# A hybrid GLA / Fourier encoder layer on one core: weight splits, scans, head fillers and the end of the scan stage in another order

## Chip, core and metric

One NeuronCore of a Trainium2 chip runs the whole layer for one sequence of 2048 positions. The metric is the device time of one execution in microseconds (us); lower is better. "The clock" is the clock that TensorE was granted, as the profile shows it, as a share of full speed.

## What is computed

```
proj = x @ w_in                      # 2048 x 1024 by 1024 x 2592, split into
q, k, v, gf_lr, gb_lr, z_gla, u, z_fnet
# A) gated linear attention, 4 heads, forward and backward, chunked; per direction
log_a = log_sigmoid(g_lr @ w_gate_up + b_gate) / 16
S_t = diag(a_t) S_{t-1} + k_t^T v_t ;  o_t = q_t S_t        # o = o_fwd + o_bwd
o = o * rsqrt(mean(o^2) + eps) * gla_norm_g * silu(z_gla)
# B) Fourier mixing: real part of the 2-D DFT over (positions, group channels)
f = real(fft2(u)) @ w_fnet * silu(z_fnet)
y = concat(o, f) @ w_out
out = layernorm(alpha * x + y, ln_g, ln_b)
```

Everything is float32. The kernel splits each large operand into a high and a low part of TensorE's fast format (`split`: a cast on ScalarE for the high part, a subtraction on VectorE for the low part) and makes three products.

## The kernel before, in words

The first stages (z_gla, u, z_fnet, the transform, q and k) end at about 397 us of the span and are not touched. Two stages follow.

**The scan stage** (`phase3`) goes through 8 blocks `b` of 256 positions, two chunks `t` of 128 each. For each block TensorE makes 96 products of x with the weights of v and the gate ranks (`pw_part`, `pv_part`: line L94), transposes the two rank tiles `rn` (`gate_t`, L813, one per chunk), and makes the gates from the transposed tile R (`gates`, L825). ScalarE and VectorE then make log-sigmoid (L827, L829, L837, L838), two running sums over positions, which are the scans of the stage's name here (`gates1`, L843 and L845 on VectorE), and from those the decays (`gates2`: small copies from L855, difference L859, clip L860, exponentials L862 and L863) that scale q (L879) and k (L880, `scaled`). With scaled q and k of the block before, `gla_a` makes the scores (L889, L890), transposes k (L893), masks the scores (L895, L896 on VectorE) and copies k back (`ks`, L898 on ScalarE); `gla_b` makes the state increments (L908, copied to `S` by L910 and L912) and the inner outputs (L915, copied by L919). The state chain over chunks runs on GpSimd (`chain_f`, `chain_step`, L1144 and L1147). x of the next block is loaded (L76) and split (`xhl`, L55 on ScalarE and L58 on VectorE).

**The last stage** (`phase4`) goes through the 16 chunks `n` from 15 down to 0: `prep` (state product L1214, squares, split `shl`), `norm` (mean square by two products L1228 and L1229, L1231 and L1232, then L1233 and the output gate L1235, split into `mix`), the output product `outp` (L1168: 24 products of 512 columns with the second half of w_out, tile wB, over the Fourier part that `p4_head` splits; 24 with the first half, tile wA) and `finish` (layer norm and store; its last step, L1264, is on GpSimd).

The second half of w_out is loaded and split in four pieces while the scan stage runs: `wof_load` is a generator, one `next(wof)` in each of blocks 2 to 6, which splits the piece loaded before and loads the next one. At the end of the scan stage `p4_start` splits the heads of chunks 15 and 14 and loads and splits the first half of w_out (`load_w`), and the Fourier part of chunk 15's output product fills the waits of `gla_a` and `gla_b` of the last block.

Each engine works through its own queue in order. The queues' order comes from the order of the code and from a scheduler that sorts by it; `after(ev)` and `issue_after` put what is inside behind the named instruction on that instruction's own engine. PSUM tiles come from rings: `mm` with 4 buffers, `pa` and `pg` with 2 each.

```
if 1 < b < 7:
    with after(self.x_dma, self.oi_ev, self.sc_ev):
        next(wof)
```

Of the kernel before, what the change touches and what calls it, by code (L numbers as in the profile page):

```python
# [43 lines left out]
class Kern:  # L44
# [7 lines left out]
    def split(self, hi, lo, src, lo_eng=None, hi_eng=None):  # L52
        nc = self.nc
        if hi_eng is None:
            nc.scalar.copy(out=hi, in_=src)  # L55
        else:
            hi_eng.tensor_copy(out=hi, in_=src)
        (lo_eng or nc.vector).tensor_tensor(out=lo, in0=src, in1=f32(hi), op=ALU.subtract)  # L58
# [12 lines left out]
    def load_x(self, b, lo_eng=None):  # L71
        nc = self.nc
        halves = []
        for hf in range(2):
# [3 lines left out]
            self.split(t[:, 0], t[:, 1], raw, lo_eng)  # L78
# [672 lines left out]
    def phase3(self):  # L751
# [16 lines left out]
        with ExitStack() as ctx:  # L768
# [82 lines left out]
            def gates2(b, blk):  # L851
# [8 lines left out]
                V.tensor_scalar(out=g8, in0=g8, scalar1=-CAP, scalar2=CAP, op0=ALU.max, op1=ALU.min)  # L860
# [22 lines left out]
            def gla_a(b, t, blk):  # L883
                q, k = blk["q"], blk["k"]
# [7 lines left out]
                for h in range(4):  # L892
                    nc.tensor.transpose(kt[:, h], k[:, h, ts_], ident)  # L893
                at = gp.tile([P, 4, P], F32, name="at", tag="at", bufs=2)
                V.tensor_tensor(out=at, in0=af, in1=mf.rearrange("p (o i) -> p o i", o=1).broadcast_to([P, 4, P]), op=ALU.mult)  # L895
                self.at_ev = V.copy_predicated(at.rearrange("p h i -> p (h i)"), mb, ab.rearrange("p h i -> p (h i)"))  # L896
                ks = gp.tile([P, 4, P], F32, name="ks", tag="ks", bufs=2)
                self.ks_ev = nc.scalar.copy(out=ks, in_=kt)  # L898
# [44 lines left out]
            for b in range(NBLK):  # L943
# [27 lines left out]
                if b == 1:  # L971
                    with after(R_ev):
                        gates2(0, prev)
                gates(b, blk)
# [46 lines left out]
    def p4_start(self, last=None):  # L1021
# [9 lines left out]
        self.wog = self.load_w("wA", a["w_out"][:, 0:4], 4, 1024)  # L1031

    def wof_load(self):
        nc = self.nc
        w = self.wof = self.wpool.tile([P, 2, 4, 1024], F32R, name="wB_w", tag="wB")
        todo = []
        for k in range(5):
            for raw, k0, c in todo:
                self.split(w[:, 0, k0, c:c + 512], w[:, 1, k0, c:c + 512], raw)
            todo = []  # L1040
            for c in (0, 512) if k < 4 else ():
# [129 lines left out]
    def phase4(self):  # L1171
        nc, a = self.nc, self.a
        V = nc.vector
        with ExitStack() as ctx:
# [12 lines left out]
            def prep(n):  # L1187
# [4 lines left out]
                d = self.blks[b]  # L1192
                if "zg" not in d:
# [11 lines left out]
                fuse = n == NCH - 1 and "op" in d  # L1205
# [20 lines left out]
            def norm(c):  # L1226
# [8 lines left out]
                zgm[c["n"]] = (V if c["n"] == NCH - 1 else nc.gpsimd).tensor_tensor(out=zg, in0=o3, in1=zg, op=ALU.mult)  # L1235
# [100 lines left out]
```

## Time and profile before

| what | value |
|---|---|
| median of 3 runs | 805.22 us (803.11 to 806.51) |
| the profiled execution | 803.78 us, span 802.0 us |
| TensorE (PE) busy | 754.5 us, 94% of the span |
| VectorE (DVE) busy | 545.2 us, 68% |
| ScalarE (ACT) busy | 382.4 us, 48% |
| GpSimd (POOL) busy | 199.4 us, 25% |
| mean granted clock | 0.986 |

The span runs from the first to the last instruction; the rest of the execution's time lies around it. Busy shares are means over stages: TensorE is full in most stages, and the idle time lies in the scan stage and at its end. Times in the rows below are us from the span's start.

### The profile page before, as it was taken

Reading aid. Unit: us, or ns where it says so; the run is one execution under the profiler, and the core shown is the slowest. Engines: PE = TensorE matmul, PEld = TensorE weight load, DVE = VectorE, ACT = ScalarE, POOL = GpSimd, SP = SyncE. Lnnn points to the kernel's source line nnn. Section 1 sums busy time; section 2 is a strip of 40 time slices with the busy share of each in tenths; the row PEclk is TensorE's granted clock in tenths of the full one; section 3 lists DMA queues with packets and bytes.
Section 4 is the critical chain, followed back from the end, with each engine's and each line's share of the span. In section 5 each row is a group of like instructions: output and inputs, shape, how many; then the busy total and the mean of one; then the engine's idle time right before and its main releaser. Section 6 shows DMA issues by size and latency. Waiting matters only on the chain.

```text
span 802.0 us, 13525 instructions
## 1 busy us (share of the span) xinstructions
PE 754.5 (94%) x5254; PEld 698.1 (87%) x5254; DVE 545.2 (68%) x802; ACT 382.4 (48%) x705; POOL 199.4 (25%) x139
## 2 busy tenths in 40 slices
PE   6999999999999998999998988899798999999994
PEld 6988899999999998999997888899677788888884
DVE  4692458555535989876576877878776767776764
ACT  6674352323224534445355776666755344334331
POOL 0000003020201000411302422432533654544431
PEclk9999999999999999999999999899999999999998
DMA  8875452443236782646764755434357445445321
GB/s 242 264 217 183 126 167 92 135 128 123 88 109 186 239 283 94 193 143 223 224 177 134 208 159 180 129 129 142 106 182 264 157 164 178 160 148 165 115 92 61
DMA packets 81407, 130.48 MB, mean 163 GB/s; under 512 B 7507, under 2 KB 55123, under 8 KB 81334
## 3 DMA queue, kind: packets, MB, share of 16 engines
q1 hardware_dynamic: 79030, 125.34, 49.4%
q10 hardware_dynamic: 2304, 4.20, 1.4%
q8 instruction: 43, 0.70, 0.4%
q14 instruction: 30, 0.25, 0.1%
HBM read 92.81 MB, written 36.70 MB: 161 GB/s over the span
## 4 chain that ended last, share of the span: by engine, by line
PE 62%; DVE 17%; ACT 9%; DMA 6%; issue 3%; POOL 2%; SPq 1%; DVEq 0%; ACTq 0%; POOLq 0%
PE mm L374 19%; PE mm L1168 19%; PE mm L291 5%; PE mm L86 4%; PE mm L94 3%; DVE c L845 3%; DVE c L843 2%; DVE fw L534 2%; DMA fw<-u_d 2%; PE pa L635 2%; PE pa L1214 1%; DVE fw L531 1%; PE pg L291 1%; PE pa L291 1%; PE mm L231 1%
## 5 line engine op out<-in xcount | busy, mean ns | idle before, releaser
L94 PE MATMUL mm<-wA_w,xhl 128*128 128x272 f32 x768 | 110.1, 300 | 0.0
L94 PEld LDWEIGHTS mm<-wA_w,xhl 128*128 128x128 f32 x768 | 103.2, 197 | 0.0
L86 PE MATMUL mm<-xhl,wC_w 128*128 128x256 f32 x768 | 96.0, 284 | 0.0
L1168 PE MATMUL mm<-wA_w,mix 128*128 128x512 f32 (+1 forms) x396 | 93.3, 385 | 2.7 <-ACT mix L55 1.6
L86 PEld LDWEIGHTS mm<-xhl,wC_w 128*128 128x128 f32 x768 | 93.7, 192 | 0.5 <-issue 0.5
L1168 PE MATMUL mm<-wB_w,mix 128*128 128x512 f32 (+1 forms) x396 | 92.3, 387 | 1.6 <-DVE mix L58 1.6
L1168 PEld LDWEIGHTS mm<-wA_w,mix 128*128 128x128 f32 x396 | 72.3, 188 | 19.2 <-ACT mix L55 2.6
L1144 POOL TENSOR_TENSOR S<-S 64x512 f32<-64x512 f32 x30 | 51.5, 1718 | 137.2 <-ACT S L910 135.4
L1168 PEld LDWEIGHTS mm<-wB_w,mix 128*128 128x128 f32 x396 | 71.5, 188 | 15.4 <-DVE mix L58 2.0
L58 DVE TENSOR_TENSOR xhl<-xraw,xhl 128x1024 fp32r<-128x1024 f32 (+1 forms) x52 | 58.0, 1118 | 27.2 <-ACT xhl L55 27.0
L55 ACT CAST xhl<-xraw 128x1024 fp32r<-128x1024 f32 (+1 forms) x52 | 49.3, 951 | 38.0 <-DMA xraw<-in_xt_dram 17.9
L55 ACT CAST x<-xraw 128x1024 fp32r<-128x1024 f32 x28 | 29.3, 1049 | 69.2 <-PE mm L374 56.9
L436 POOL TENSOR_TENSOR t<-t,t 128x512 f32<-128x512 f32 x7 | 10.8, 1556 | 190.2 <-DVE t L428 122.2
L58 DVE TENSOR_TENSOR x<-xraw,x 128x1024 fp32r<-128x1024 f32 x28 | 37.8, 1352 | 29.1 <-ACT x L55 29.1
L1264 POOL TENSOR_TENSOR r<-r,lnb 128x1024 f32<-128x1024 f32 x15 | 36.1, 2409 | 80.3 <-issue 56.7
L670 POOL TENSOR_TENSOR yf<-yf,zfl 128x256 f32<-128x256 f32 x24 | 21.5, 923 | 119.5 <-ACT yf L649 110.8
L374 PE MATMUL mm<-wC_s,x 128*128 128x256 f32 x384 | 48.2, 283 | 0.0
L1147 POOL TENSOR_TENSOR S<-S,alpha 64x512 f32<-64x512 f32 x30 | 47.4, 1580 | 2.7 <-ACT alpha L932 0.4
L374 PEld LDWEIGHTS mm<-wC_s,x 128*128 128x128 f32 x384 | 47.1, 192 | 0.1
L291 PE MATMUL mm<-xhl,wA_w 128*128 128x512 f32 x192 | 43.9, 389 | 0.0
L291 PEld LDWEIGHTS mm<-xhl,wA_w 128*128 128x128 f32 x192 | 36.0, 188 | 7.4
L55 ACT CAST mix<-zg 128x512 fp32r<-128x512 f32 x16 | 9.9, 622 | 57.2 <-POOL zg L1235 55.9
(202 smaller groups left out, 1489.2 us busy)
## 6 DMA issues: line engine op xcount, KB each, us to landing
xraw<-in_xt_dram SPq DMA_DIRECT2D x48, 512.0 KB, 4.6
xr<-in_x_dram SPq DMA_DIRECT2D x16, 512.0 KB, 3.8
out_dram<-r SPq DMA_DIRECT2D x15, 512.0 KB, 2.9
xraw<-in_xt_dram SPq DMA_DIRECT2D x24, 256.0 KB, 4.2
zg_d<-zs SPq DMA_DIRECT2D x32, 128.0 KB, 3.7
u_d<-t SPq DMA_DIRECT2D x16, 256.0 KB, 3.1
zf_d<-t SPq DMA_DIRECT2D x16, 256.0 KB, 2.5
zfl<-zf_d SPq DMA_DIRECT2D x32, 128.0 KB, 3.7
```

Source lines behind the costliest of these rows:

```text
L55: nc.scalar.copy(out=hi, in_=src)
L58: (lo_eng or nc.vector).tensor_tensor(out=lo, in0=src, in1=f32(hi), op=ALU.subtract)
L86: mm = self.nc.tensor.matmul(ps, w[:, s, k, c0:c0 + P], x[:, m, k % 4, :], start=(k == 0 and i == 0), stop=(k == KB - 1 and i == 2))
L94: self.nc.tensor.matmul(ps, x[:, s, k % 4, t * P:(t + 1) * P], w[:, m, k, c0:c0 + cols], start=(k == 0 and i == 0), stop=(k == KB - 1 and ...
L291: nc.tensor.matmul(ps[c], self.wzg[:, s, 2 * q + kk, c * P:(c + 1) * P], x[:, m, kk], start=(q == 0 and kk == 0 and j == 0), stop=(q == 3 ...
L374: nc.tensor.matmul(ps[:, i], s_[s][:, k, i * P:(i + 1) * P], m_[m][:, k], start=(k == 0 and j == 0), stop=(k == 3 and j == 2))
L670: (nc.gpsimd if g < 3 else nc.vector).tensor_tensor(out=yb, in0=yb, in1=zf, op=ALU.mult)
L845: V.tensor_tensor_scan(out=c2[64:128, ::-1], data0=r2[64:128, ::-1], data1=g2[64:128, ::-1], initial=0.0, op0=ALU.mult, op1=ALU.add)
L1144: E.tensor_tensor(out=S[ds, dst], in0=S[ds, dst], in1=S[ds, src], op=ALU.add)
L1147: E.tensor_tensor(out=d3, in0=d3, in1=al, op=ALU.mult)
L1168: nc.tensor.matmul(y, c["mix"][:, s, eb], w[:, v, eb % 4, lo:lo + m], start=(eb == 4 and i == 0), stop=(eb == 3 and i == 2))
L1264: nc.gpsimd.tensor_tensor(out=r, in0=r, in1=lnb, op=ALU.add)
```

## The change

Line numbers in this section are those of the file named with them. The parts of the change:

- `wof_load` now yields three times for a piece: after the load, after the two casts (ScalarE), after the two subtractions (VectorE). The load stands behind the x load of blocks 2 to 5, the casts behind the last `ks` copy at the head of blocks 3 to 6, the subtractions behind the x split of blocks 3 to 6.
- `gates1` (from L837 on) stands behind the masks and the `ks` copy of `gla_a(b-1, 0)`; in block 1 the first `gla_a` comes ahead of it.
- `gates2` is cut in two: `gates2` ends with the clip, `gates3` begins with the exponentials. `gla_a` is cut in two: `gla_s` (scores, transposes, `ks`), `gla_m` (masks).
- In block 7, where there is no next x to load, `p4_start` runs: the heads of chunks 15 and 14 are split there.
- The end of the scan stage: the Fourier part of chunk 15's output product comes first, the masks of chunk 13 stand behind the clip, the first half of w_out is loaded behind the last `ks` and the scaled k, half of chunk 14's Fourier part follows.
- In `phase4`: half of chunk 13's Fourier part is made early, into a `pa` buffer; chunk 15's gate tile is loaded early, into the free half of `oi`; chunk 14's output gate is on VectorE instead of GpSimd; for chunk 15 the square on ScalarE comes ahead of the copy on VectorE.

```diff
-                V.tensor_scalar(out=g8, in0=g8, scalar1=-CAP, scalar2=CAP, op0=ALU.max, op1=ALU.min)
+                self.clip_ev = V.tensor_scalar(out=g8, in0=g8, scalar1=-CAP, scalar2=CAP, op0=ALU.max, op1=ALU.min)
+
+            def gates3(b, blk):
+                g, c, g8, c8 = blk["gc"]
                 eq = c
...
             def gla_a(b, t, blk):
+                gla_s(b, t, blk)
+                gla_m(blk)
...
                 pw_part(xh, 0, blk)
                 if b > 1:
                     gla_b(b - 2, 0 if b == 2 else 1, old)
+                if 2 < b < 7:
+                    with after(self.ks_ev):
+                        next(wof)
...
-                if b + 1 < NBLK:
-                    with self.tc.issue_after(self.rn_ev.ins):
+                with after(self.rn_ev):
+                    if b + 1 < NBLK:
                         xn = self.load_x(b + 1)
-                if 1 < b < 7:
-                    with after(self.x_dma, self.oi_ev, self.sc_ev):
+                    else:
+                        self.p4_start(blk)
+                if 2 < b < 7:
+                    with after(self.x_lo):
+                        next(wof)
+                if 1 < b < 6:
+                    with after(self.x_dma):
                         next(wof)
...
                 if b > 1:
                     gla_a(b - 1, 0, prev)
-                if b == 1:
-                    with after(self.sc_ev):
+                    with after(self.ks_ev, self.at_ev):
                         gates1(b, blk)
-                else:
+                elif b == 0:
                     gates1(b, blk)
...
-                if b:
-                    gla_a(b - 1, min(b - 1, 1), prev)
+                if b == 1:
+                    gla_a(0, 0, prev)
+                    with after(self.ks_ev, self.at_ev):
+                        gates1(b, blk)
+                elif b:
+                    gla_s(b - 1, 1, prev)
+                    if b < NBLK - 1:
+                        gla_m(prev)
                 old, prev = prev, blk
             b = NBLK
-            with after(self.ks_ev, self.at_ev):
+            h15, h14 = self.head[NCH - 1], self.head[NCH - 2]
+            self.outp(h15, [4, 5, 6, 7], (0,))
+            with after(self.ks_ev):
                 gates2(b - 1, prev)
+            with after(self.clip_ev):
+                gla_m(old)
+            with after(self.ks_ev):
+                gates3(b - 1, prev)
+            self.outp(h15, [4, 5, 6, 7], (1,))
             gla_b(b - 2, 1, old)
             self.chain_f(2 * b - 3, 2 * b - 1)
-            with after(self.ks_ev):
-                self.p4_start(prev)
-            h15, h14 = self.head[NCH - 1], self.head[NCH - 2]
-            self.outp(h15, [4, 5, 6, 7], (0,))
             gla_a(b - 1, 0, prev)
-            self.outp(h15, [4, 5, 6, 7], (1,))
+            with after(self.sc_ev, self.ks_ev):
+                self.wog = self.load_w("wA", a["w_out"][:, 0:4], 4, 1024)
+            self.outp(h14, [4, 5, 6, 7], (0,))
             gla_a(b - 1, 1, prev)
             gla_b(b - 1, 0, prev)
+            nc.sync.dma_start(out=prev["oi"][:, 1].rearrange("p (h j) -> p h j", h=4), in_=self.zg_d[b - 1][:, :, P:2 * P])
...
-                zgm[c["n"]] = (V if c["n"] == NCH - 1 else nc.gpsimd).tensor_tensor(out=zg, in0=o3, in1=zg, op=ALU.mult)
+                zgm[c["n"]] = (V if c["n"] >= NCH - 2 else nc.gpsimd).tensor_tensor(out=zg, in0=o3, in1=zg, op=ALU.mult)
...
+            h13 = self.head[NCH - 3] = self.p4_head(NCH - 3)
+            self.outp(h13, [4, 5, 6, 7], (0,), get=self.pa)
             norm(cur)
```

The order of the built instructions, at three places.

**Blocks 3 to 6, VectorE.** The rows around the second rank tile: L880 scales k, L783 is the rank tile's low part, `wB_w` the w_out piece, `xhl` the x split, L811 belongs to R. Before:

```order
L880 TENSOR_TENSOR g<-kr,g 128x1024
L58 TENSOR_TENSOR wB_w<-wraw,wB_w 128x512 x2
L783 TENSOR_TENSOR rn<-mm,rn 128x32
L58 TENSOR_TENSOR xhl<-xraw,xhl 128x1024 x2
L811 MEMSET R 2x256
```

Of the change (L883 is the k scaling there, L1080 the subtraction of a w_out piece):

```order
L883 TENSOR_TENSOR g<-kr,g 128x1024
L783 TENSOR_TENSOR rn<-mm,rn 128x32
L58 TENSOR_TENSOR xhl<-xraw,xhl 128x1024 x2
L1080 TENSOR_TENSOR wB_w<-wraw,wB_w 128x512 x2
L811 MEMSET R 2x256
```

The two subtractions went from ahead of the rank tile to behind the x split. On ScalarE the two casts, which stood ahead of the rank tile's casts (L781, L782), now stand between the second `ks` copy and the small copies of the scan's results:

```order
L804 COPY v<-mm 128x272
L902 COPY ks<-pg 128x512
L1077 CAST wB_w<-wraw 128x512 x2
L855 COPY cmid<-c 128x8
L857 COPY cend<-c 64x8
```

**Block 1, VectorE.** The masks of chunk 0 (`at`) and the scans (`c`). Before:

```order
L880 TENSOR_TENSOR g<-kr,g 128x1024
L838 SCALAR_TENSOR_TENSOR g<-mm,g 128x512 x2
L895 TENSOR_TENSOR at<-pa,mf 128x512
L843 SCALAR_TENSOR_TENSOR c<-rst,g 64x1024
L845 SCALAR_TENSOR_TENSOR c<-rst,g 64x1024
L896 COPY_PREDICATED at<-mb,pa 128x512
L783 TENSOR_TENSOR rn<-mm,rn 128x32
```

Of the change (L908 and L909 are the masks there):

```order
L883 TENSOR_TENSOR g<-kr,g 128x1024
L908 TENSOR_TENSOR at<-pa,mf 128x512
L909 COPY_PREDICATED at<-mb,pa 128x512
L838 SCALAR_TENSOR_TENSOR g<-mm,g 128x512 x2
L843 SCALAR_TENSOR_TENSOR c<-rst,g 64x1024
L845 SCALAR_TENSOR_TENSOR c<-rst,g 64x1024
L783 TENSOR_TENSOR rn<-mm,rn 128x32
```

The second mask went from behind both scans to ahead of them. In blocks 2 to 7 both masks of chunk 0 stood ahead of the scans already.

**The end of the scan stage, TensorE**, from the last block's chunk 0 (`v,ks` and `at,v`) to the first norm (`shl,ones`). Before:

```order
L908 MATMUL pg<-v,ks 128x128 x4
L915 MATMUL pg<-at,v 128x128 x4
L1168 MATMUL mm<-wB_w,mix 128x512 x2
L1017 MATMUL pg<-fone,fm 1x1
L1168 MATMUL mm<-wB_w,mix 128x512 x2
L908 MATMUL pg<-v,ks 128x128 x4
L915 MATMUL pg<-at,v 128x128 x4
L1214 MATMUL pg<-qp,S 128x128 x4
L1168 MATMUL mm<-wB_w,mix 128x512 x19
L1228 MATMUL pg<-shl,ones 128x512
```

Of the change (L1204 is the output product there, L1252 the state product, L1266 the norm's):

```order
L919 MATMUL pg<-v,ks 128x128 x4
L926 MATMUL pg<-at,v 128x128 x4
L1204 MATMUL mm<-wB_w,mix 128x512 x7
L1049 MATMUL pg<-fone,fm 1x1
L1204 MATMUL mm<-wB_w,mix 128x512 x2
L919 MATMUL pg<-v,ks 128x128 x4
L926 MATMUL pg<-at,v 128x128 x4
L1204 MATMUL mm<-wB_w,mix 128x512 x3
L1252 MATMUL pg<-qp,S 128x128 x4
L1204 MATMUL pa<-wB_w,mix 128x512 x12
L1266 MATMUL pg<-shl,ones 128x512
```

Ahead of the first norm there are now 12 products of chunk 13 (`pa`) in place of 19 of chunks 15 and 14, which have moved further ahead: of the 48 of chunks 15 and 14, 36 stand ahead of the first row shown, against 25 before.

## Rows read from the trace of the kernel before

**Rows 1.** Windows between L813's starts: length, busy us of each engine, clock, DMA.

```profile
469.42:493.66 24.24, 21.31 (x175) 20.53 (x176) 18.78 (x24) 15.99 (x37) 8.37 (x4) 0.92 0.50 153
517.78:542.72 24.94, 22.57 (x175) 21.59 (x176) 18.65 (x24) 16.16 (x37) 7.80 (x4) 0.88 0.50 149
542.72:563.47 20.75, 19.91 (x175) 19.12 (x176) 16.96 (x21) 13.97 (x34) 7.58 (x4) 1.00 0.46 145
563.47:626.48 63.01, 55.06 (x345) 45.50 (x346) 45.87 (x66) 35.64 (x67) 28.59 (x19) 1.00 0.52 175
```

**Rows 2.** Timeline, TensorE at L813: start, length, instruction, idle before and releaser.

```profile
469.42 0.45 PE L813 MATMUL mm<-ident,rn 128*96 128x128 f32 x1 [3.15 <-DVE rn L783]
...
493.66 0.45 PE L813 MATMUL mm<-ident,rn 128*96 128x128 f32 x1 [2.93 <-DVE rn L783]
493.76 3.01 PE L94 MATMUL mm<-wA_w,xhl 128*128 128x272 f32 x12
...
542.72 0.32 PE L813 MATMUL mm<-ident,rn 128*96 128x128 f32 x1 [2.37 <-DVE rn L783]
542.79 1.76 PE L94 MATMUL mm<-wA_w,xhl 128*128 128x272 f32 x12
...
563.47 0.32 PE L813 MATMUL mm<-ident,rn 128*96 128x128 f32 x1 [0.84 <-DVE rn L783]
```

**Rows 3.** Timeline, ScalarE, VectorE and SyncE around L813 of block 4.

```profile
491.00 1.14 ACT L55 CAST wB_w<-wraw 128x512 fp32r<-128x512 f32 x2
491.65 1.85 DVE L58 TENSOR_TENSOR wB_w<-wraw,wB_w 128x512 fp32r<-128x512 f32 x2 [1.54 <-ACT wB_w L55]
493.42 0.18 DVE L783 TENSOR_TENSOR rn<-mm,rn 128x32 fp32r<-128x32 f32 x1
...
496.62 0.90 SPq L1043 DMA_DIRECT2D wraw<-in_w_out_dram  x2
```

**Rows 4.** Timeline, ScalarE and VectorE in block 6.

```profile
542.69 0.36 ACT L797 COPY v<-mm 128x240 f32<-128x240 f32 x1 [0.39 <-DVE rn L783]
542.95 1.05 ACT L55 CAST xhl<-xraw 128x1024 fp32r<-128x1024 f32 x1
544.04 1.23 DVE L58 TENSOR_TENSOR xhl<-xraw,xhl 128x1024 fp32r<-128x1024 f32 x1 [0.24 <-ACT xhl L55]
549.46 2.28 DVE L843 TENSOR_TENSOR_SCAN c<-rst,g 64x1024 f32<-64x1024 uint8 x1
553.24 0.59 ACT L898 COPY ks<-pg 128x512 f32<-128x512 f32 x1 [1.29 <-PE pg L893]
554.99 0.21 ACT L855 COPY cmid<-c 128x8 f32<-128x8 f32 x1 [1.16 <-DVE c L845]
563.00 0.19 ACT L782 CAST rn<-mm 128x32 fp32r<-128x32 f32 x1
```

**Rows 5.** The tile wB_w, blocks 3 to 6: ns min/median/max.

```profile
L58 DVE TENSOR_TENSOR wB_w<-wraw,wB_w x8: 676/956/1255, 467.4 to 541.9; 128x512 fp32r<-128x512 f32 x8
```

**Rows 6.** Timeline, VectorE and TensorE in block 1 and at L813 of block 2.

```profile
429.16 2.27 DVE L843 TENSOR_TENSOR_SCAN c<-rst,g 64x1024 f32<-64x1024 uint8 x1
433.77 0.73 DVE L896 COPY_PREDICATED at<-mb,pa 128x512 f32<-128x512 uint8 x1
434.64 1.61 PE L915 MATMUL pg<-at,v 128*128 128x128 f32 x8 [3.19 <-DVE rn L783]
442.84 0.38 PE L813 MATMUL mm<-ident,rn 128*96 128x128 f32 x2
```

**Rows 7.** Timeline, the end of the scan stage and the first chunks of the last.

```profile
580.65 2.14 DVE L58 TENSOR_TENSOR mix<-mf,mix 128x512 fp32r<-128x512 f32 x2
585.38 0.37 PE L889 MATMUL pa<-qp,g 64*128 64x128 f32 x1 [0.51 <-DVE g L880]
...
607.96 0.73 PE L1168 MATMUL mm<-wA_w,mix 128*128 128x512 f32 x2 [1.41 <-ACT mix L55]
```

**Rows 8.** The tile wraw, blocks 3 to 6: from issue to landing.

```profile
DMA to landing us min/median/max: 5.7/5.7/5.9
```

More of the change, by code (lines that the diff above doesn't have):

```diff
@@ L57, in split @@
             hi_eng.tensor_copy(out=hi, in_=src)
-        (lo_eng or nc.vector).tensor_tensor(out=lo, in0=src, in1=f32(hi), op=ALU.subtract)
+        return (lo_eng or nc.vector).tensor_tensor(out=lo, in0=src, in1=f32(hi), op=ALU.subtract)
     def load_w(self, tag, src, nkb, cols, eng=None):
@@ L77, in load_x @@
             t = self.xpool.tile([P, 2, 4, BLK], F32R, name="xhl", tag="xhl", bufs=4)
-            self.split(t[:, 0], t[:, 1], raw, lo_eng)
+            self.x_lo = self.split(t[:, 0], t[:, 1], raw, lo_eng)
             halves.append(t)
@@ L893, in gla_a, with gla_m @@
                     nc.tensor.transpose(kt[:, h], k[:, h, ts_], ident)
+                ks = gp.tile([P, 4, P], F32, name="ks", tag="ks", bufs=2)
+                self.ks_ev = nc.scalar.copy(out=ks, in_=kt)
+                blk["sc"] = af, ab, ks
+            def gla_m(blk):
+                af, ab, ks = blk.pop("sc")
                 at = gp.tile([P, 4, P], F32, name="at", tag="at", bufs=2)
@@ L896, in gla_a @@
                 self.at_ev = V.copy_predicated(at.rearrange("p h i -> p (h i)"), mb, ab.rearrange("p h i -> p (h i)"))
-                ks = gp.tile([P, 4, P], F32, name="ks", tag="ks", bufs=2)
-                self.ks_ev = nc.scalar.copy(out=ks, in_=kt)
                 blk["ak"].append((at, ks))
@@ L973, in phase3 @@
                         gates2(0, prev)
+                        gates3(0, prev)
                 gates(b, blk)
@@ L1030, in p4_start @@
         self.head = {n: self.p4_head(n) for n in (NCH - 1, NCH - 2)}
-        self.wog = self.load_w("wA", a["w_out"][:, 0:4], 4, 1024)
+        if not last:
+            self.wog = self.load_w("wA", a["w_out"][:, 0:4], 4, 1024)
     def wof_load(self):
@@ L1035, in wof_load @@
         w = self.wof = self.wpool.tile([P, 2, 4, 1024], F32R, name="wB_w", tag="wB")
[L1036 to L1041, printed above, removed]
+        for k in range(4):
+            raws = []
+            for c in (0, 512):
                 raw = self.xpool.tile([P, 512], F32, name="wraw", tag="wraw", bufs=4)
                 nc.sync.dma_start(out=raw, in_=self.a["w_out"][:, 4 + k, c:c + 512])
-                todo.append((raw, k, c))
+                raws.append((raw, w[:, 0, k, c:c + 512], w[:, 1, k, c:c + 512]))
+            yield
+            for raw, hi, lo in raws:
+                nc.scalar.copy(out=hi, in_=raw)
+            yield
+            for raw, hi, lo in raws:
+                nc.vector.tensor_tensor(out=lo, in0=raw, in1=f32(hi), op=ALU.subtract)
             yield
@@ L1163, in outp @@
         if ebs[0] >= 4:
-            c.setdefault("y", []).extend((self.mm([P, cuts[i][1]]), *cuts[i]) for i in halves)
+            c.setdefault("y", []).extend(((get or self.mm)([P, cuts[i][1]]), *cuts[i]) for i in halves)
         for y, lo, m in c["y"][halves[0]:halves[-1] + 1]:
@@ L1192, in prep @@
                 d = self.blks[b]
+                fuse = n == NCH - 1 and "op" in d
                 if "zg" not in d:
@@ L1204, in prep @@
                         self.chain_step(n, n + 1, n + 1, 1)
-                fuse = n == NCH - 1 and "op" in d
+                if fuse:
+                    zg = oi.rearrange("p (h j) -> p h j", h=4)
                 o = p4.tile([P, 512], F32, name="o4", tag="o4", bufs=2)
@@ L1215, in prep @@
                 if fuse:
+                    nc.scalar.activation(out=sq, in_=ip, func=AF.Square)
                     V.tensor_copy(out=o, in_=ip)
-                    nc.scalar.activation(out=sq, in_=ip, func=AF.Square)
                 else:
@@ L1273, in phase4 @@
                 nxt = prep(n - 1) if n > 0 else None
+                if n == NCH - 3:
+                    self.outp(cur, [4, 5, 6, 7], (1,))
                 if "y" not in cur:
```

8 lines of the change are left out of this document (6 added, 2 removed).

## Prediction, made before the changed kernel ran

> **What bounds the kernel now.** The page's shares come first: TensorE is busy for 94% of the span, so only its idle time and its slow time can be won. The table of windows then says where these lie. Between the starts of the rank transposes L813 the blocks take 24.24 and 24.94 us with 21.31 and 22.57 us of busy TensorE, at clocks of 0.92 and 0.88; the block that starts at 542.72 takes 20.75 with 19.91 busy at 1.00; and the stretch from 563.47 to 626.48, the end of the scan stage and the first chunks of the last, takes 63.01 with 55.06 busy [rows 1]. The reader should see two losses: idle time, and work that takes longer because the clock is lower.
>
> The timeline at L813 shows the cause in a block. TensorE stands there for 3.15, 2.93 and 2.37 us, each time for the rank tile's low part L783, but only for 0.84 us at 563.47, the block in which no piece of w_out is split [rows 2]. Behind the wait at 493.66 the twelve products of L94 take 3.01 us, behind that at 542.72 they take 1.76 [rows 2]: so after a wait of 2.9 us the clock had fallen (1.2 in place of 2.4 GHz for a while), after one of 2.4 it had not, and a fall costs at least 3.01 - 1.76 = 1.25 us. What L783 waits for is one look further: the two casts of wB on ScalarE (1.14 us from 491.00) and the two subtractions on VectorE (1.85 us from 491.65) stand directly ahead of it, and L783 itself takes 0.18 [rows 3].
>
> Two places differ. In block 1 both scans stand ahead of the second mask L896, which starts only at 433.77 though the first scan began at 429.16; L915 waits 3.19 us meanwhile [rows 6]. At the end of the stage VectorE splits chunk heads for 2.14 us (580.65) ahead of the scaled k, and the last block's scores L889 wait for that k until 585.38; the products with wA wait another 1.41 us at 607.96 [rows 7].
>
> **The wB splits, blocks 3 to 6.** Removed from ahead of L783 are 1.14 us on ScalarE and 1.85 on VectorE, which overlap in part [rows 3]. Nothing else stands between the products and L783 than in the block at 563.47, so I take that block's wait, 0.84, as what is left [rows 2]. That is also the bound below: it waits for its own casts and L783.
>
> The two casts go behind the second `ks` copy, which ends at 553.24 + 0.59 = 553.83 in block 6, and ahead of L855, which starts at 554.99 after 1.16 us of idle ScalarE waiting for the second scan [rows 4]. The casts take 1.14 [rows 3], so they just fit and cost nothing, if the raw piece is there. It is issued 496.62 - 493.66 = 2.96 us after L813 [rows 2, 3] and lands 5.9 later at worst [rows 8], so 8.9 us after L813; the slot begins at 553.83 - 542.72 = 11.1. There are 2.2 us to spare. Without that cover L855 and all the gates behind it come late by what is missing.
>
> The subtractions go behind the x split, so ahead of the scan. One takes between 676 and 1255 ns, median 956 [rows 5]. I take the short end, because at the new place GpSimd's state chain of that block has not begun; the long end adds 4 x (0.956 - 0.676), so some 1.1 us for two subtractions in two blocks, and 2.2 for all four blocks. The Trainium skill's "GPSIMD Engine Reference", section 1 (Specifications), says that GpSimd shares its SBUF interfaces with VectorE and that instructions with two SBUF inputs, as these are, contend; the spread in the row agrees, and by that rule the sum below would be up to 2.2 us higher if the chain did overlap them.
>
> What is late next is the scan. In block 6 the second x cast starts at 542.95 and ends at 544.00, 1.28 us after L813 [rows 2, 4]. Behind the change it can't run under the wait, since the wait is gone: the rank casts end 0.28 us ahead of L813 (563.00 + 0.19 against 563.47), then come a cast of 1.05, the copy of v of 0.36 and a cast of 1.05 [rows 2, 4], which ends at 2.18. So R and the x split come 0.9 us later, and the two subtractions of 0.68 fill VectorE's time up to the masks; both ways the scan begins about 0.86 us later than the 549.46 - 542.72 = 6.74 us of block 6 [rows 2, 4]. From the scan to the next L813 it was 563.47 - 549.46 = 14.0 us [rows 2, 4], and I keep that. The new period is 20.75 + 0.86 = 21.6. Its bounds are 19.91, TensorE's busy time with no wait at all [rows 1], and 21.6 + 1.25 + 0.56 = 23.4, with the clock still falling and two contended subtractions.
>
> Four periods, from the L813 at 469.42 to that at 563.47, took 94.05 us [rows 1]; they will take 4 x 21.6 = 86.4: **-7.65**. The wait at 469.42 itself falls from 3.15 to 0.84 [rows 2]: **-2.3**.
>
> **Masks ahead of the scans in block 1.** The wait of 3.19 at L915 goes, and with it the half clock behind it, which shows in L915's 1.61 us; at the price of a fall from above, 1.25, this is **-4.4** up to the L813 at 442.84 [rows 6]. The scans begin some 0.7 us later (the mask's 0.73), which ScalarE and VectorE have time for. Bounds: -3.2, if the clock falls for another reason, and -4.4.
>
> **The end of the stage.** Splitting the heads in block 7 instead of there takes 2.14 us off the way to the scaled k [rows 7]; in block 7 no x is split, whose cast and subtraction, 1.05 and 1.23 apiece [rows 4], leave room. I take 2.14 for it, and the 1.41 at 607.96 for fillers that are made earlier and a mix that is ready [rows 7]: **-3.55**. Some of it comes back: the first norm has 12 fillers for 19, GpSimd's last step of the layer norm still precedes chunk 13's mix, and the copies of the state stand behind casts of wA that wait for a load. The gate tile loaded early, chunk 14's gate on VectorE and the order of chunk 15's square are part of the same preparation; I give them nothing of their own. The bounds are nothing and the whole idle of the stretch, 63.01 - 55.06 = 7.95 [rows 1]. From chunk 13 on TensorE has no gaps, so nothing behind 626.48 hides or adds to it.
>
> **The sum.** -7.65 - 2.3 - 4.4 - 3.55 = -17.9. The profiled execution took 803.78, so it becomes 785.9; the median lies 1.44 above that execution, so I forecast **787 us**. A difference of 0.5%, 4 us, is what a measurement here can tell from none.
>
> **Rivals.** *The clock still falls.* The waits become shorter but several, and the two levels lie close: 2.93 us brought a fall, 2.37 none [rows 2]. One fall in each of four periods adds 4 x 1.25 = 5: 792. For it speaks that the blocks now run at 0.88 to 0.92, against it the block at 1.00 with a wait of 0.84 at its end [rows 1]. The Trainium skill, "TensorE: Matmul & The Clock Gate", section "HAM oscillation", describes kernels whose every burst begins cold after a gap; by it the blocks stay cold only if a long gap is left in each, and the row at 1.00 agrees that short ones do no harm.
>
> *The end gives nothing*, because the last block's gates and not the splits set it: 787 + 3.55, so 791. The wait for k of only 0.51 at 585.38 [rows 7] speaks for it.
>
> *The wait only moves.* R and the scan come later than worked out, and the blocks stay near 24 us: -7.65 and -2.3 are lost, 797. Against it: block 7's wait is 0.84 with the same gates [rows 2].
>
> *Slower: the raw piece is late at its new cast.* ScalarE works in order; casts that wait for the load hold L855, so the decays, the scaled k and the next scores. Beyond the spare 2.2 us each us costs 4 over four blocks. The 17.9 are used up at 17.9 / 4 = 4.5 us, so with a landing 6.7 us later than the 5.9 shown, some 12.6 [rows 8]; at 5.5 us late the time is 809. Against it stand landings of 5.7 to 5.9 in all blocks, though the x load and two others are queued beside it.
>
> **How the numbers follow.** Forecast 0.64 (its own range 781 to 791, from the bounds of tail and contention), the end gives nothing 0.10, the clock still falls 0.11, the wait moves 0.05, late piece 0.10, half of which ends within 0.5% and half slower. So faster 0.90, same 0.05, slower 0.05. The range: downward four periods with half of the 6.8 us between 21.6 and 19.91 and the other half of the end's idle (4.4) give 787 - 7.8 = 779; upward it takes in the first three rivals, to 797. What is left out, 0.10 above and a little below, is within 2 in 10.
>
> **What would show it.** Waits at L813 of blocks 3 to 6 of at most 1.5 us, products of 1.76 behind them and a clock of 1.00; periods near 21.6; no wait of 3 us at L915 in block 1, and L813 of block 2 near 438; the L813 of block 7 near 549; from there to chunk 13's wA products about 59.5 us instead of 63.01; casts of wB that start as `ks` ends, and L855 right behind. Wrong would be: ScalarE idle ahead of the wB casts with a DMA as releaser, a new wait ahead of the scores L889 or of R's products L825 as long as the one removed, or subtractions of wB above 1 us beside GpSimd's chain.

## The result, and the profile after

| | before | changed |
|---|---|---|
| median | 805.87 us (803.11 to 809.94, 4 runs) | 792.8 us (787.95 to 794.35, 4 runs) |
| ratio, 95% interval | | 0.984 (0.9807 to 0.9873) |
| profiled execution, span | 803.78 us, 802.0 us | 794.35 us, 792.6 us |
| TensorE busy, clock | 754.5 us, 0.986 | 751.7 us, 0.990 |

Faster by 1.6%, inside the range, 5.8 us above the forecast of 787. The forecast's own range, 781 to 791, does not hold it. In the changed kernel's rows L896 and L897 are the scores L889 and L890, L919 and L926 the state increments and inner outputs L908 and L915, L908 and L909 the masks L895 and L896, L1180 and L1183 GpSimd's state chain L1144 and L1147, L1204 the output product, L1266 the norm's, L1273 the output gate L1235, L1302 the layer norm's last step L1264; lines up to L855 keep their numbers.

The windows between L813's starts of the changed kernel (length, busy us of TensorE, its weight loads, VectorE, ScalarE, GpSimd; clock, DMA share, GB/s):

```profile
467.51:489.10 21.59, 20.15 (x174) 19.14 (x174) 18.22 (x23) 15.95 (x37) 8.52 (x5) 1.00 0.55 172
489.10:510.69 21.59, 20.14 (x174) 19.14 (x174) 18.22 (x23) 15.95 (x37) 8.54 (x5) 1.00 0.55 171
532.28:553.90 21.62, 20.13 (x174) 19.13 (x175) 18.16 (x23) 14.91 (x35) 8.54 (x5) 1.00 0.57 171
553.90:621.15 67.25, 58.73 (x357) 48.42 (x358) 49.76 (x71) 37.19 (x70) 28.89 (x19) 0.97 0.56 179
```

The blocks answer to [rows 1]: 21.6 us at clock 1.00 where 24.2 and 24.9 at 0.92 and 0.88 stood. The last row runs from L813 of block 7 to the norm product of chunk 12. The same stretch of the kernel before:

```profile
563.47:630.14 66.67, 58.20 (x358) 47.78 (x358) 48.59 (x69) 37.04 (x70) 30.62 (x20) 1.00 0.51 174
```

So the end of the stage gained nothing: 67.25 against 66.67. The timeline of TensorE at the places of [rows 2, 6]:

```profile
434.27 1.06 PE L926 MATMUL pg<-at,v 128*128 128x128 f32 x8
441.36 0.66 PE L813 MATMUL mm<-ident,rn 128*96 128x128 f32 x2
460.75 1.13 PE L926 MATMUL pg<-at,v 128*128 128x128 f32 x8 [1.27 <-DVE at L909]
467.51 0.31 PE L813 MATMUL mm<-ident,rn 128*96 128x128 f32 x1 [1.01 <-DVE rn L783]
489.10 0.32 PE L813 MATMUL mm<-ident,rn 128*96 128x128 f32 x1 [0.96 <-DVE rn L783]
553.90 0.32 PE L813 MATMUL mm<-ident,rn 128*96 128x128 f32 x1 [1.00 <-DVE rn L783]
```

The waits at L813 are 0.96 to 1.01, and the products of block 1 wait no more. New is 1.27 us in block 2. The wB pieces at their new places (timeline of ScalarE and VectorE in a block, then the tile's subtractions, min/median/max):

```profile
500.35 0.59 ACT L902 COPY ks<-pg 128x512 f32<-128x512 f32 x1 [1.29 <-PE pg L900]
500.83 1.14 ACT L1077 CAST wB_w<-wraw 128x512 fp32r<-128x512 f32 x2
502.25 0.20 ACT L855 COPY cmid<-c 128x8 f32<-128x8 f32 x1 [0.28 <-DVE c L845]
...
492.28 1.29 DVE L1080 TENSOR_TENSOR wB_w<-wraw,wB_w 128x512 fp32r<-128x512 f32 x2
496.72 2.28 DVE L843 TENSOR_TENSOR_SCAN c<-rst,g 64x1024 f32<-64x1024 uint8 x1
...
L1080 DVE TENSOR_TENSOR wB_w<-wraw,wB_w x8: 684/684/686, 470.7 to 536.1; 128x512 fp32r<-128x512 f32 x8
```

The casts start behind `ks` and leave 0.28 of the old 1.16 us that ScalarE waited for the second scan [rows 4]; the subtractions take the short end of [rows 5] eight times of eight. The scan begins 496.72 - 489.10 = 7.62 us after L813, where 7.60 was worked out. Issue and casts of the fourth piece (SyncE, ScalarE):

```profile
492.99 0.93 SPq L1073 DMA_DIRECT2D wraw<-in_w_out_dram  x2
522.42 1.14 ACT L1077 CAST wB_w<-wraw 128x512 fp32r<-128x512 f32 x2
```

The four pieces are issued at 430.18, 449.34, 471.40 and 492.99 and cast at 456.10, 479.24, 500.83 and 522.42, so each is cast 26 to 30 us after its issue. At the end of the stage (TensorE, then GpSimd):

```profile
573.47 0.37 PE L896 MATMUL pa<-qp,g 64*128 64x128 f32 x1 [1.02 <-DVE tf L941]
595.03 1.13 PE L1252 MATMUL pa<-qp,S 128*128 128x128 f32 x8 [0.83 <-POOL S L1180]
597.68 0.73 PE L1204 MATMUL mm<-wA_w,mix 128*128 128x512 f32 x2 [0.88 <-ACT mix L55]
616.08 0.73 PE L1204 MATMUL pa<-wA_w,mix 128*128 128x512 f32 x2 [1.74 <-ACT mix L55]
617.34 3.98 PE L1204 MATMUL pa<-wA_w,mix 128*128 128x512 f32 x10 [0.53 <-DVE mix L58]
...
611.50 2.65 POOL L1302 TENSOR_TENSOR r<-r,lnb 128x1024 f32<-128x1024 f32 x1 [11.95 <-DVE r L1301]
614.12 1.25 POOL L1273 TENSOR_TENSOR zg<-o,zg 128x512 f32<-128x512 f32 x1
```

The scores come 573.47 - 553.90 = 19.6 us after L813, against 585.38 - 563.47 = 21.9 before [rows 2, 7]: 2.3 sooner, where 2.14 was forecast. But in place of the 1.41 at 607.96 [rows 7] TensorE now waits 0.83 for the state chain on GpSimd and 0.88 for the mix. Chunk 13's products with wA wait 1.74 and 0.53 us, its gate stands on GpSimd behind the layer norm's step of 2.65 us, and the ten products behind the waits take 3.98 us. The same products of the kernel before:

```profile
626.48 0.73 PE L1168 MATMUL mm<-wA_w,mix 128*128 128x512 f32 x2 [0.20 <-ACT mix L55]
627.74 2.56 PE L1168 MATMUL mm<-wA_w,mix 128*128 128x512 f32 x10 [0.52 <-DVE mix L58]
```

The clock of this place in the changed kernel, and of one in stages that the change does not touch (windows):

```profile
618.00:620.00 2.00, 2.00 (x6) 1.58 (x5) 1.40 (x3) 1.16 (x1) 0.18 (x1) 0.50 0.68 258
...
344.00:346.00 2.00, 2.00 (x11) 2.00 (x11) 2.00 (x6) 1.32 (x2) 0.00 (x0) 0.50 0.24 91
```

The second belongs to a wait of 3.71 us of TensorE in the transform, where the kernel before waited 1.02 and 1.47:

```profile
342.06 1.01 PE L655 MATMUL pg<-yhl,wcs 128*128 128x256 f32 x3 [3.71 <-DVE yf L662]
```

It makes L813 of block 0 begin 3.5 us later (409.61 for 406.13). By stretch, L813 to L813, after less before:

| stretch | before | after | difference | forecast |
|---|---|---|---|---|
| start to block 0 | 406.13 | 409.61 | +3.48 | 0 |
| block 0 to 2 | 36.71 | 31.75 | -4.96 | -4.4 |
| block 2 to 3 | 26.58 | 26.15 | -0.43 | -2.3 |
| block 3 to 7 | 94.05 | 86.39 | -7.66 | -7.65 |
| block 7 to norm of chunk 12 | 66.67 | 67.25 | +0.58 | -3.55 |
| from there to the end | 171.86 | 171.45 | -0.41 | 0 |
| sum | 802.0 | 792.6 | -9.4 | -17.9 |

### The profile page after: what moved, and what is told of

Read it like the earlier page. It is cut to its first block, busy times and chain, and to the rows that moved or that the text cites. A ratio compares the mean times of both kernels' runs of the same rounds, so it can differ in the third digit from the quotient of the medians.

```text
span 792.6 us, 13524 instructions
## 1 busy us (share of the span) xinstructions
PE 751.7 (95%) x5254; PEld 694.9 (88%) x5254; DVE 540.5 (68%) x803; ACT 382.2 (48%) x705; POOL 198.3 (25%) x138
## 4 chain that ended last, share of the span: by engine, by line
PE 62%; DVE 19%; ACT 10%; DMA 4%; issue 3%; SPq 1%; POOL 0%; DVEq 0%; ACTq 0%; POOLq 0%
PE mm L1204 19%; PE mm L374 19%; PE mm L291 5%; PE mm L86 5%; DVE c L845 3%; DVE c L843 2%; PE pa L635 2%; DMA fw<-u_d 2%; ACT xhl L55 2%; DVE fw L534 1%; PE pa L1252 1%; DVE fw L531 1%; PE pg L291 1%; PE pa L291 1%; PE mm L94 1%
## 5 line engine op out<-in xcount | busy, mean ns | idle before, releaser
L94 PE MATMUL mm<-wA_w,xhl 128*128 128x272 f32 x768 | 105.1, 292 | 0.0
L94 PEld LDWEIGHTS mm<-wA_w,xhl 128*128 128x128 f32 x768 | 98.6, 189 | 0.0
L1204 PE MATMUL mm<-wA_w,mix 128*128 128x512 f32 (+1 forms) x384 | 89.8, 384 | 1.1 <-ACT mix L55 0.9
L1204 PE MATMUL mm<-wB_w,mix 128*128 128x512 f32 (+1 forms) x384 | 89.4, 387 | 0.0
L1204 PEld LDWEIGHTS mm<-wA_w,mix 128*128 128x128 f32 x384 | 70.4, 188 | 15.9 <-ACT mix L55 1.2
L1180 POOL TENSOR_TENSOR S<-S 64x512 f32<-64x512 f32 x30 | 49.7, 1657 | 125.8 <-ACT S L921 123.6
L1204 PEld LDWEIGHTS mm<-wB_w,mix 128*128 128x128 f32 x384 | 69.3, 188 | 13.0
L1302 POOL TENSOR_TENSOR r<-r,lnb 128x1024 f32<-128x1024 f32 x15 | 36.3, 2419 | 86.8 <-issue 51.2
L1183 POOL TENSOR_TENSOR S<-S,alpha 64x512 f32<-64x512 f32 x30 | 49.3, 1645 | 2.4
L374 PE MATMUL mm<-x,wB_s 128*128 128x256 f32 x288 | 36.3, 283 | 0.0
```

The source lines that it names most:

```text
L94: self.nc.tensor.matmul(ps, x[:, s, k % 4, t * P:(t + 1) * P], w[:, m, k, c0:c0 + cols], start=(k == 0 and i == 0), stop=(k == KB - 1 and ...
L374: nc.tensor.matmul(ps[:, i], s_[s][:, k, i * P:(i + 1) * P], m_[m][:, k], start=(k == 0 and j == 0), stop=(k == 3 and j == 2))
L1180: E.tensor_tensor(out=S[ds, dst], in0=S[ds, dst], in1=S[ds, src], op=ALU.add)
L1183: E.tensor_tensor(out=d3, in0=d3, in1=al, op=ALU.mult)
L1204: nc.tensor.matmul(y, c["mix"][:, s, eb], w[:, v, eb % 4, lo:lo + m], start=(eb == 4 and i == 0), stop=(eb == 3 and i == 2))
L1302: nc.gpsimd.tensor_tensor(out=r, in0=r, in1=lnb, op=ALU.add)
```

## Experiments

Ratios are to the kernel before, run beside each. The theory after the result: two parts did what they should, the end is undone by the order on GpSimd, and GpSimd's overlap with VectorE takes the rest, in block 2. **The parts alone.** First, the kernel before with the wB splits moved:

```diff
+                if 2 < b < 7:
+                    with after(self.ks_ev):
+                        next(wof)
...
-                if 1 < b < 7:
-                    with after(self.x_dma, self.oi_ev, self.sc_ev):
+                if 2 < b < 7:
+                    with after(self.x_lo):
+                        next(wof)
+                if 1 < b < 6:
+                    with after(self.x_dma):
                         next(wof)
```

> The kernel before with one part alone: load, casts and subtractions of the w_out pieces at their new places, all else as before. Theory (the splits ahead of the rank tile make the waits at L813): the waits at L813 in blocks 3 to 6 fall from 2.4-3.2 us to about 1.0, no half clock behind them, T3 to T7 (the L813 at 469.42 to that at 563.47, 94.05 us) takes 86 to 87 us, L915 of block 1 still waits about 3 us, the end of the stage is as before (66.7 us from T7 to the norm product of chunk 12); total 794 to 797. Rival (the wait only moves to R or the scores): periods stay near 24 us and the total at 803 to 806.

794.51 us, 0.9868 (0.9833 to 0.9902). Blocks 3 to 7 took 554.21 - 467.83 = 86.38 us, with waits of 0.96 to 1.01 (L813 on TensorE's timeline):

```profile
467.83 0.32 PE L813 MATMUL mm<-ident,rn 128*96 128x128 f32 x1 [1.01 <-DVE rn L783]
554.21 0.32 PE L813 MATMUL mm<-ident,rn 128*96 128x128 f32 x1 [1.00 <-DVE rn L783]
```

The rival that the wait only moves is out. The end of the stage took 621.79 - 554.21 = 67.58 us instead of the 66.7 expected; the clock fell to 0.50 in it, near 601. Second, block 1's masks alone:

```diff
-                if b == 1:
-                    with after(self.sc_ev):
-                        gates1(b, blk)
-                else:
+                if b != 1:
                     gates1(b, blk)
...
+                if b == 1:
+                    gla_a(0, 0, prev)
+                    with after(self.ks_ev, self.at_ev):
+                        gates1(b, blk)
```

> The kernel before with one part alone: in block 1 the masks of chunk 0 come ahead of the scans. Theory: the 3.19 us wait at L915 and the half clock behind it go, T0 to T2 (36.7 us between the L813 of blocks 0 and 2) becomes 31.5 to 32.5, the rest is as before; total 800 to 802. Rival (the later scan makes L825 or the next scores late by as much): T0 to T2 stays above 35 us, total 804 to 806.

800.84 us, 0.9953 (0.9934 to 0.9973); blocks 0 to 2 took 436.65 - 404.91 = 31.74, and 2 to 3 took 464.07 - 436.65 = 27.42, 0.84 more than before: some comes back in block 2. "The rest is as before" missed in one more point: three later waits at L813 were 2.42 to 2.44 instead of 2.93, 2.96 and 2.37, and blocks 3 to 7 took 92.27 us instead of 94.05. Behind two of these waits the clock still fell, though only about 1.4 us after TensorE had begun again (a window behind the wait that ends at 487.93):

```profile
490.00:492.00 2.00, 2.00 (x15) 1.77 (x15) 0.74 (x2) 1.91 (x5) 0.00 (x0) 0.50 0.89 276
```

Third, the end alone: the changed kernel with `wof_load`, its calls and block 1 of before.

> The kernel before with the parts at the end of the scan stage and in the last stage alone (heads in block 7, masks behind the clip, w_out load and fillers in the new order, 12 products of chunk 13 ahead of the first norm, gate of chunk 14 on VectorE); wB splits and block 1 as before. Theory (chunk 13's gate on GpSimd behind the layer norm's last step, with 24 products of cover in place of 36, takes back what the earlier heads gave): L889 of the last block comes 2.2 us sooner behind T7, but chunk 13's first wA product waits 1.5 to 2 us, the clock falls to half behind it, and T7 to the norm product of chunk 12 takes 66.5 to 67.5 us as before (66.67); total 804 to 807. Rival (the end's order does gain, and the gain shows in a run without a clock fall in the first stages): 63 to 64 us there and 801 to 802 in total.

805.33 us, 1.0014 (0.9985 to 1.0043): nothing, as the theory has it, and 632.99 - 565.73 = 67.26 us in the stretch, with the same wait (L1194 is the output product here):

```profile
629.34 0.73 PE L1194 MATMUL pa<-wA_w,mix 128*128 128x512 f32 x2 [1.74 <-ACT mix L55]
630.60 2.56 PE L1194 MATMUL pa<-wA_w,mix 128*128 128x512 f32 x10 [0.52 <-DVE mix L58]
```

Here the ten products took 2.56 behind the same waits, so the clock did not fall there. It fell at two other places of the stretch, and the scores came 586.01 - 565.73 = 20.28 us after L813, 1.6 sooner than before instead of 2.2:

```profile
588.00:590.00 2.00, 2.00 (x6) 1.52 (x6) 1.62 (x3) 2.00 (x4) 0.20 (x1) 0.50 0.28 104
612.00:614.00 2.00, 2.00 (x6) 1.57 (x6) 1.07 (x3) 1.62 (x4) 0.00 (x0) 0.50 0.38 98
```

So the half clock at chunk 13 belongs to one execution, while 67.1 to 67.3 us for the stretch came in all three profiles of this end, each with a fall somewhere. The three parts alone gain 10.2, 3.9 and -0.6 us, in sum 13.4; the whole change gained 13.1, and 14.0 when it was measured again below.

**Why the end gives nothing.** The changed kernel, with chunk 13's gate on VectorE (`>= NCH - 3` for `>= NCH - 2`):

> The changed kernel with one edit: chunk 13's output gate on VectorE instead of GpSimd. Theory: the wait of 1.74 us at chunk 13's first wA product and the half clock behind it go; T7 to the norm product of chunk 12 falls from 67.25 to 63.5 to 64.5 us; about 3 us below the changed kernel, 788 to 790 in a run with a clock fall in the first stages and 785 to 787 in one without. Rival (something else than the gate, the S chain or the mixed Fourier part, holds chunk 13): the wait stays above 1 us and the stretch above 66.

790.83 us, 0.9817 (0.9782 to 0.9852), but the stretch was 620.09 - 554.35 = 65.74 and a wait of 1.08 stayed: half a miss, with neither the theory's 63.5 to 64.5 nor the rival's 66. The clock was 1.00 in the whole stretch. The rows (GpSimd, VectorE, TensorE) say why:

```profile
612.63 2.65 POOL L1302 TENSOR_TENSOR r<-r,lnb 128x1024 f32<-128x1024 f32 x1 [9.08 <-DVE r L1301]
...
613.52 2.31 DVE L1273 TENSOR_TENSOR zg<-o,zg 128x512 f32<-128x512 f32 x1
...
616.54 0.74 PE L1204 MATMUL pa<-wA_w,mix 128*128 128x512 f32 x2 [1.08 <-ACT mix L55]
```

The gate began while GpSimd's step ran, and took 2.31 us; it ended at 615.83, 0.55 after the step (615.28). Next, the last steps of chunk 15's layer norm (`finish2`, cut out of `finish`) behind chunk 13's gate; on GpSimd first, then with the gate on VectorE:

```diff
+                if late and n == NCH - 2:
+                    with ExitStack() as es:
+                        for e in (zgm[NCH - 3], self.rs):
+                            es.enter_context(self.tc.issue_after(e.ins))
+                        finish2(*late.pop())
```

> The changed kernel with one edit: the last steps of chunk 15's layer norm (scale on ScalarE, product on VectorE, sum on GpSimd, store) are issued behind chunk 13's output gate, which stays on GpSimd. Theory (it is the queue order, the layer norm's step of 2.65 us ahead of the gate on GpSimd and its product of 1.23 us ahead of the gate on VectorE, not the engine of the gate): the wait of 1.74 us at chunk 13's first wA product goes to under 0.4 us, no half clock behind it; T7 (L813 of block 7) to the norm product of chunk 12 falls from 67.25 to about 63.5 us; total 787 to 790. Rival (the gate on GpSimd is itself too slow): a wait of 1 us or more stays, stretch above 65.5.

791.42 us, 0.9852 (0.9818 to 0.9885), above the 787 to 790 expected. Chunk 13's wait is gone and the norm product of chunk 12 begins after 615.56 - 551.30 = 64.26, but the second one behind it waits 1.58 for its split: the gate, the state chain and the layer norm's step now run on GpSimd one behind the other, and VectorE's instructions beside them are long (a mix subtraction 2.20 us). The gain is passed on as a new wait.

> As the run before it, with chunk 13's gate on VectorE as well. Theory (in the run with the gate alone, VectorE's gate took 2.31 us because GpSimd's 2.65 us step ran beside it): behind the gate that step no longer overlaps it, the gate takes about 0.7 us, no wait at chunk 13's first wA product, T7 to the norm product of chunk 12 63 to 63.5 us; total 786 to 790. Rival (contention has nothing to do with the 2.31 us): the gate still takes over 1.5 us.

788.04 us, 0.98 (0.9779 to 0.982), and 614.55 - 550.87 = 63.68. VectorE's gate, with nothing on GpSimd until 610.03 (L1310 is the layer norm's last step here):

```profile
607.98 0.69 DVE L1273 TENSOR_TENSOR zg<-o,zg 128x512 f32<-128x512 f32 x1
...
610.03 2.65 POOL L1310 TENSOR_TENSOR r<-r,lnb 128x1024 f32<-128x1024 f32 x1 [9.95 <-DVE r L1309]
...
611.84 2.88 PE L1204 MATMUL pa<-wA_w,mix 128*128 128x512 f32 x12
```

0.69 for 2.31, and no wait. Against the kernel before the stretch gains 66.67 - 63.68 = 2.99 of the 3.55 us that the prediction gave the end. Against the changed kernel it is 3.57 less, but part of that is the clock, which was 1.00 in the whole stretch here. The run with the gate alone, also at 1.00, took 65.74, so the order on GpSimd and VectorE is worth 2.06 at the same clock, of which 0.50 goes again in the next chunk (12.31 against 11.81 us from norm to norm). In the median the gain is 2.6 us (790.66 for the changed kernel on the same chip, below). Whether the new order also keeps the clock up is not shown. Next, the second half of w_out's first half later:

```diff
+            with after(self.oi_ev, self.at_ev):
+                self.load_w("wA", a["w_out"][:, 0:4], 4, 1024, None, self.wog, (2, 3))
```

> As the run before it, with the second half of the load and split of w_out's first half (wA) behind the state and output copies of the last block's chunk 0. Theory (the state copies S stand behind wA casts that wait for loads on ScalarE, which makes TensorE wait 0.58, 0.98 and 0.63 to 1.69 us between L889 of the last block and the first norm): those waits fall by 1 to 2 us in sum, T7 to the norm product of chunk 12 61.5 to 62.5 us; total 785 to 789. Rival (wA comes too late for chunk 15's first products, or the state chain on GpSimd bounds): no change or 1 to 2 us longer.

786.47 us, 0.9781 (0.9763 to 0.9799): the lowest median, 1.6 below the run before it, though single executions of the two overlap. From the scores to the first norm 587.52 - 569.52 = 18.00 us, against 19.61 in the run before (570.44 to 590.05), although the clock was 0.91 there, against 1.00; the waits for the state copies are gone. The whole stretch, 62.94, is a little above what was expected, with a second fall of the clock behind it (0.50 at 594 to 596). The changed kernel again, on the same chip:

> The changed kernel itself once more, beside the other three on one chip. Expected as at first: 788 to 794; waits of 0.96 to 1.01 us at L813 in blocks 3 to 7, 1.74 at chunk 13. What is asked: whether the wait of 3.71 us at L655 near 342 us, in stages that the change does not touch, comes in this execution again (then L813 of block 0 near 409.6) or not (then near 406); one theory says that it belongs to chance in when a transfer lands, since the kernel before and the runs with a part alone did not have it and the order there is the same.

790.66 us, 0.9829 (0.9813 to 0.9846); 1.74 at chunk 13, 1.26 in block 2, and in the transform 0.57 and 1.45 instead of 3.71:

```profile
345.82 0.62 PE L655 MATMUL pg<-yhl,wcs 128*128 128x256 f32 x3 [1.45 <-DVE yf L662]
```

Of twelve profiles two had the 3.71, both of the changed kernel or a variant of it. In the first of them the transform's input landed later and VectorE's work beside GpSimd was longer (L522 1.80 us for 1.22); why it landed later stays open.

**GpSimd beside VectorE.** In block 2 of the changed kernel the mask is late because the scan ahead of it took 3.41 us (in the kernel with the masks alone it began as late, 11.3 us after L813, took 2.28, and L915 did not wait):

```profile
452.66 3.41 DVE L843 TENSOR_TENSOR_SCAN c<-rst,g 64x1024 f32<-64x1024 uint8 x1
...
452.64 1.28 POOL L1180 TENSOR_TENSOR S<-S 64x512 f32<-64x512 f32 x1 [3.04 <-ACT S L921]
454.00 2.90 POOL L1183 TENSOR_TENSOR S<-S,alpha 64x512 f32<-64x512 f32 x1
```

A first kernel, the fastest with a tiny copy on GpSimd that reads the scan's result ahead of the chain, was to hold the chain back:

> As the seventh kernel, with GpSimd's state chain of blocks 2 to 7 held behind the block's second scan: GpSimd first copies one column of the scan's result (a new tiny instruction), so it can't start before the scan ends. Theory (the scan L845 takes 3.20 us beside GpSimd's chain and 2.29 us alone in blocks 0 and 1, and L843 of block 2 takes 3.4 in place of 2.28 for the same reason): both take 2.3 us in blocks 2 to 7, the wait at L915 of block 2 (1.26 us) goes, and T3 to T7 falls from 86.4 to 83 to 84 us, T2 to T3 from 26.1 to 24 to 25; total about 782. Rival (the overlap only moves, on to the masks, L859 and the scaled q and k, which then take longer): scans of 2.3 us but periods of 21.3 us or more, total 785 to 790. Second rival (the scan's length has nothing to do with GpSimd): still 3.20.

787.4 us, 0.9798 (0.9766 to 0.983): the chain's steps still ran beside the scan (493.67 to 499.4), so it told nothing. With the steps tied to the copy (L844 and L846 are the scans here, L1184 and L1187 the chain, L939 and L943 small differences ahead of the scaled q and k):

```diff
+                    tok_ev = nc.gpsimd.tensor_copy(out=tok, in_=blk["gc"][1][:, 0, 0:1])
+                    with after(tok_ev):
+                        self.chain_f(2 * b - 3, 2 * b - 1)
```

> The run before this one left the chain where it was: the scheduler put the chain's steps ahead of the copy on GpSimd, so it tested nothing. Here the steps are tied behind that copy on GpSimd's queue. Theory (a scan takes longer because GpSimd's steps run beside it): L843 and L845 take about 2.3 us each in blocks 2 to 7, the steps run after the scan; whether the time falls is the second question. If the overlap costs nothing at its new place, T3 to T7 falls from 86.4 to 82 to 84 us and the total to about 782; rival (the cost only moves to the masks, L859 and the scaled q and k beside which the steps now run): those take longer, periods of 21.3 us or more, total 785 to 790. If the scan's 3.20 stays with GpSimd idle beside it, contention is not its cause.

793.82 us, 0.9878 (0.9847 to 0.991), which is 6 to 7 us slower than the two kernels before it. VectorE and GpSimd in a block:

```profile
497.57 2.29 DVE L846 TENSOR_TENSOR_SCAN c<-rst,g 64x1024 f32<-64x1024 uint8 x1
502.45 1.00 DVE L939 TENSOR_TENSOR cend<-cend,cmid 128x8 f32<-128x8 f32 x1
503.98 1.25 DVE L939 TENSOR_TENSOR cst<-cst,cmid 128x8 f32<-128x8 f32 x1
505.31 1.03 DVE L943 TENSOR_TENSOR tf<-cend,cmid 64x8 f32<-64x8 f32 x1
...
499.93 0.18 POOL L999 COPY tok<-c 128x1 f32<-128x1 f32 x1 [16.21 <-DVE c L846]
500.06 1.29 POOL L1184 TENSOR_TENSOR S<-S 64x512 f32<-64x512 f32 x1
501.43 2.00 POOL L1187 TENSOR_TENSOR S<-S,alpha 64x512 f32<-64x512 f32 x1
```

All scans take 2.28 or 2.29 now, so the overlap is what made them 3.20, and in block 2 the wait at L915 is gone; but three instructions of some 0.16 us elsewhere take 1.0 to 1.25 beside the chain, ahead of the scaled q and k. The first two end at 503.45 and 505.23, just as a step of the chain does (503.43 and 505.20): they wait for it. Blocks 3 to 7 took 555.28 - 464.64 = 90.64. The rival was right that the cost moves, and it was larger than the 785 to 790 that it gave: the new place is nearer the path.

## Why the prediction was right, and where it was off

*The wB splits*: right to the second decimal, and shown by the first kernel alone: 4 periods of 21.6, no fall of the clock in them, casts in ScalarE's gap, subtractions at the short end, the scan 0.9 later. So close a hit is in part luck, since a fall of the clock alone moves a block by more than a microsecond. The rivals of a clock that still falls, of a wait that moves and of a late raw piece did not come. The spare time of 2.2 us for the raw piece was misread: it takes the piece issued in a block for the one cast 8 us later, but it is cast at least one block later (the fourth piece of the kernel before, issued at 496.62 [rows 3], at 540.05). In the changed kernel 26 to 30 us lie between issue and cast, and the pieces landed after 4.9 to 7.5 us, so some 18 us were to spare. The lateness that would make the kernel slower was not tried.

*Masks in block 1*: -4.96 for -4.4, the second kernel -4.97, beyond the stated bounds of -3.2 to -4.4. The price of the fall was too small: 1.25 counts twelve products, while the clock of the kernel before was 0.78, 0.50 and 0.86 in the windows of 2 us from 434 to 440. By an estimate from these shares that cost 0.44 + 1.00 + 0.28 = 1.7 us, and 3.19 + 1.7 = 4.9.

*The wait at 469.42, "-2.3"*: it fell by 2.14, but block 2 gave 1.7 back: R's products waited 0.78 for 0.24, and L915 1.27 behind a scan of 3.41 us. The step that failed is that the two parts leave block 2 alone. The masks alone gave back 0.84 there, with R's products at 0.78 and the scans as before; the other 0.87 came only with both parts together, where GpSimd's chain starts at 452.64, just ahead of the scan at 452.66. The Trainium skill, "GPSIMD Engine Reference", section 1 (Specifications), says that GpSimd shares its SBUF interfaces with VectorE and that VectorE's instructions with two SBUF inputs contend; the scan has two, and 2.28 against 3.41 us agrees. The prediction weighed that rule for the wB subtractions, which run clear of the chain at their new place (684 ns each), and not for the scan.

*The end, "-3.55"*: this term was lost, as the rival "the end gives nothing" had it, though not for that rival's reason. The 2.14 for the scores did come. The 1.41 at 607.96 did not: 0.83 and 0.88 stand in its place. And the prediction listed "GpSimd's last step of the layer norm still precedes chunk 13's mix" among what comes back and gave it no price; with 24 products of cover instead of 36 it cost 1.74 + 0.53 of wait against 0.20 + 0.52 before, and 3.98 - 2.56 = 1.4 of half clock in this execution. In two other profiles of this end half clock came elsewhere in the stretch, which took 67.26 and 67.13. With that order mended and the gate beside nothing, the stretch was 63.68, 3.0 below 66.67.

*The untouched stages* added 3.5 us in the profiled execution. Without that the sum gives 803.78 - 9.4 - 3.5 = 790.9, as the second measurement has it (median 790.66, profile 791.13). That the mechanism of the first two parts is right is shown; that 792.8 lies in the range is owed to the rivals, which widened it to 797, while the end was lost for a reason that the forecast had named and not priced.

## What to carry to other kernels

Move what an engine does ahead of the critical instruction into a gap that the rows show, count the new start of the next long instruction to the tenth, and the block's period follows. When filler products are moved forward, look at the wait that they covered where they stood, and price every instruction queued ahead of that wait's releaser. Work on GpSimd is not free because GpSimd is idle: ask beside which VectorE instruction it will run, and which of the two starts first.

## What the runs showed of the hardware

- The scan of 64x1024 takes 2.28 us alone and 2.97 to 3.41 when it starts during a step of GpSimd's chain (64x512). The steps take 1.28 and 1.03 alone and 1.9 to 3.1 when they start during a scan. A 128x512 product took 0.69 alone and 2.31 when it started during a step of 2.65 us, 128x8 differences 0.16 alone and 1.0 to 1.25.
- In these pairs the one that started first kept its length and the other ended about its own length, or less, after it. The step at 452.64 kept 1.28 and the scan at 452.66 took 3.41; the scan at 496.72 kept 2.28, and the step that began at 497.37 ended at 500.07, 1.07 after the scan. So it is a wait for the other to end, not a slowdown of both.
- The clock fell to 0.50 behind waits of 2.93 to 3.19 and 3.71 us, at once or about 1.4 us later, and stayed at 1.00 behind the waits of 0.94 to 1.06 at L813 in the changed kernel and its variants. Between these a wait's length does not decide it: behind waits of 2.37 to 2.44 it fell in two cases (2.42 and 2.44, the kernel with the masks alone) and not in four, in the last kernel behind 1.85 and 2.12 and not behind 1.78 and 1.98, and behind 1.74 + 0.53 it fell in one execution (ten products 3.98 us) and not in two others (2.56 and 2.57).
